# A place of its own for the fourth copy of a run's product sums, and the loads and sums that form z spread over the plain units

## The chip, the cores and the metric

The kernel runs on one core of one Trainium2 chip. The metric is the device time of one execution in microseconds (us); of several executions the median is taken. TensorE multiplies, VectorE and ScalarE work elementwise and empty the accumulator memory (PSUM), POOL (GpSimd) and SP issue transfers, and 16 DMA engines carry them. In the profile's rows PE is TensorE's matmuls, PEld its loading of the stationary operand, DVE is VectorE and ACT is ScalarE.

## What is computed

One layer of a hybrid decoder trunk on 512 positions of width 2048: a mixer of gated linear attention and mLSTM heads, then a feed-forward block with squared ReLU, both with a residual, a conditioning vector and a layer norm. The part that matters here is the end:

```python
def _sq_relu_mlp(u, w_ff1, w_ff2):
    return jnp.square(jax.nn.relu(u @ w_ff1)) @ w_ff2
...
        x = _layer_norm(ALPHA * x + g2 * y, ln2_g[l], ln2_b[l])
```

The hidden width is 8192, all data is float32. A float32 product is made of three products of rounded parts: each operand is split into hi (rounded) and lo (the rest), and hi·hi + hi·lo + lo·hi are accumulated.

## The kernel before, in words

The change lies in the second feed-forward product, from about 1500 to 2188 us: the hidden matrix h (kept in device memory as `hd`) times `w_ff2`. Its 8192 rows of depth are cut into pairs of 128-row tiles, the output's 2048 columns into four blocks b of 512 (`NCB`, `CB`). The list `units` sets the order of work; one unit is one pair times one block.

*Seven-product units* (kind "S", 96 of them, numbers 0 to 95). The first 24 pairs are multiplied by Strassen's scheme in Winograd's form: seven products of half-size operands in place of eight. `w_operands` (L1180 to L1198) makes a unit's weight operands: SP loads a raw weight tile into one of three buffers, ScalarE rounds a part of it (L1190, tiles named bh), VectorE forms combinations (`w_combos`, L1164 to L1167), ScalarE rounds those (L1194, hi), VectorE subtracts (L1197, bl; L1198, lo). This is done two units ahead (`LOOK`). `h_operands` makes a pair's seven operands of h (L1273 to L1284); they stay for as long as the pair is in use. `seven` (L1430 on) has 42 matmuls of 256 columns, six for each product, in the order 1, 2, 3, 7, 5, 6, 4 (`ORDER`).

Units come in 15 runs: run r works on block (r + 1) mod 4 with up to four groups of two pairs, so that the runs have 2, 4, 6, then nine times 8, then 6, 4 and 2 units. In the trace the runs begin at about 1500.1, 1511.5, 1538.1, 1574.9, 1615.3, 1657.7, and so on to 1974.5 (six units), 2008.3 (four) and 2030.8 (two). The seven products of a run are summed in seven of eight PSUM banks. At its end `evac` (L1452) copies them out: ScalarE copies two at a time into a staging place (L1457, seven copies into four places in turn), and a transfer carries each place to the block's `sums` in device memory: the first four runs write them plainly from SP's queue (L1462), later ones add to what is there, with accumulating transfers from POOL's queue (L1460). The staging places are three, used in rotation by `scratch("st", 2, 3)`: half-blocks of z that have no content yet. So the fourth staging of a run (product 4 alone) goes to the place of its first.

*Plain units* (kind "C", 24, numbers 96 to 119). The last pairs are multiplied without the scheme: six units a block, 24 matmuls of 512 columns each, from 2046.3 us on. Weights and h are split by `split` (L125, L126). In these units the function `at(n, fn)` puts side jobs ahead of unit n's matmuls, in the order in which they were registered: `sums_load` (L1469, seven loads of 256 KB from `sums` into tiles q), `z_sums` (L1471, seven operations of VectorE that turn a block's seven sums into its four quarters of z, in two steps), loads of the residual (`last_load`, L1403) and its scaling (`last_x2`, L1421 and L1422), layer-norm rows (`ln_rows`, L1122), the tail's operands (`tail_h`, `tail_w`) and, behind a block's last unit, the addition of its plain products to z (L1525) and `last_z` (L1426, L1427). Block 0's sums are loaded at unit 96 and summed at 97 and 98, block 1's at 99 to 101, block 2's at 102 to 104, block 3's at 105 to 107.

The tiles q, the residual, and 24 of the operands of eight pairs come from one ring of 28 places of 2 KB a partition (`f3_slot`, `NS`). The raw-weight buffers also take the layer-norm rows and the tail's raw tiles.

Order: `tc.manual_schedule(engines=MANUAL)` (L712) keeps VectorE and ScalarE in the order in which the source issues to them. TensorE, SP and POOL get their order from the planner, which may put an instruction ahead of others that it thinks late.

Of the kernel before, what the change touches and what calls it, by code (L numbers as in the profile page):

```python
# [13 lines left out]
ALU = mybir.AluOpType  # L14
# [3 lines left out]
S = 512  # L18
# [7 lines left out]
NCB = D // CB  # L26
# [32 lines left out]
def trunk_layer_kernel(  # L59
# [5 lines left out]
    V, A, T, G = nc.vector, nc.scalar, nc.tensor, nc.gpsimd  # L65
# [10 lines left out]
    def mm_bank(name, shape=(P, CB)):  # L76
        turns["mm"].append(turns["mm"].pop(0))
        kind = turns["mm"][-1]
        return psum.tile(list(shape), F32, tag=kind, bufs=6 if kind == "mm" else 2, name=name)
# [586 lines left out]
    for n, (i, g, k) in enumerate(units):  # L666
# [5 lines left out]
        if at_ == 0:  # L672
            gen = ada_start(*nxt) if nxt else iter(())
            steps = 4 * nxt[1] + 1 if nxt else 0
# [252 lines left out]
    st = zp.tile([P, NT, NCB, 6], F32, name="st")  # L927
    ab = zp.tile([P, 2, KT], F32, name="ab")

    def blk(b):  # L930
        return slice(b * CB, (b + 1) * CB)
# [134 lines left out]
    def f1_units(halves, banks, first=None, ahead=None):  # L1066
        for kp in range(KP):
# [23 lines left out]
    zs_ = [z[:, b, 2 * i:2 * i + 2].rearrange("p t c -> p (t c)")  # L1091
           for b in range(NCB) for i in range(2)]
    turn = {}

    def scratch(what, at, n):
        turn[what] = (turn.get(what, -1) + 1) % n
        return zs_[at + turn[what]]
# [21 lines left out]
    def ln_rows(g_ap, b_ap, b, name, tag="raw"):  # L1119
        gb = strm.tile([P, 2, CB], F32, tag=tag, bufs=3, name=name)  # L1120
        for i, ap in enumerate((g_ap, b_ap)):
            nc.sync.dma_start(gb[:, i, :], ap[0:1, blk(b)].broadcast_to([P, CB]))  # L1122
        return gb
# [46 lines left out]
    def halves(t):  # L1170
        return t.rearrange("p (e t) -> p e t", e=2)
# [57 lines left out]
    ORDER = (1, 2, 3, 7, 5, 6, 4)  # L1229
# [75 lines left out]
    NU = len(units)  # L1305
# [5 lines left out]
    def at(n, fn):  # L1311
        jobs.setdefault(n, []).append(fn)
# [5 lines left out]
    def prepare2(n):  # L1318
        if n < len(units):
            kind, b, ft, _, _ = units[n]  # L1320
            name = f"f2_{b}_{ft}"
            if kind == "S":
                ahead.append(w_operands(w_ff2, ft * P, b * CB, name, waiting, f1_slot))
            else:
                ahead.append(w_plain(ft * P, b * CB, name))


    for p in range(GP, SP + CP):
        use = [u[2] for u in units].index(2 * p)
        n = max(1, use - 6 + 3 * (p % 2)) if p < SP else NU - 10 + 2 * (p - SP)  # L1330
# [21 lines left out]
    for nb in range(2, DFF // CB):  # L1352
        pb = {m: mm_bank(f"fp{nb}_{m}", (P, 2, HB)) for m in ORDER}
# [44 lines left out]
    def f3_slot(name):  # L1398
        return ff3.tile([P, S], F32, tag="s", bufs=NS, name=name)

    def last_load(b, x2, t):
        x2.append(f3_slot(f"x2_{b}_{t}"))
        nc.sync.dma_start(x2[t], xd[t * P:(t + 1) * P, blk(b)])  # L1403
# [3 lines left out]
    def tail_h(i):  # L1407
        for h, l in h_operands("C", tail + 2 * i, "ssss"):
            act[0].append(h)
            act[1].append(l)  # L1410

    def tail_w(b, i):
        raw = raw_unit(w_ff2, (tail + 2 * i) * P, b * CB, CB, f"wl{b}_{i}")
        for t in range(2):
            V.tensor_tensor(raw[:, t, :], raw[:, t, :], g2b[b], ALU.mult)
        for t in range(2):
            w2[b, 2 * i + t] = h_split(raw[:, t, :], "hl", f"wl{b}_{i}_{t}_")


    def last_x2(x2, gb, t):  # L1420
        V.tensor_tensor(x2[t], x2[t], gb[:, 0, :], ALU.mult)  # L1421
        V.tensor_tensor(x2[t], x2[t], gb[:, 1, :], ALU.add)  # L1422

    def last_z(b, x2, t):
        zs = z[:, b, t]
        V.tensor_tensor(zs, zs, g2b[b], ALU.mult)  # L1426
        V.scalar_tensor_tensor(zs, x2[t], ALPHA, zs, ALU.mult, ALU.add)  # L1427
# [21 lines left out]
    sums = [hdram.tile([P, 7 * S], F32, name=f"sums{b}") for b in range(NCB)]  # L1449
    begun = set()  # L1450

    def evac(pb, b):  # L1452
        for i in range(0, 7, 2):
            ms = ORDER[i:i + 2]
            st_ = scratch("st", 2, 3)[:, :len(ms) * S]
            for e, m in enumerate(ms):
                A.copy(halves(st_[:, e * S:(e + 1) * S]), pb[m])  # L1457
            o = sums[b][:, i * S:(i + len(ms)) * S]
            if b in begun:
                G.dma_start(o, st_, accum_op=ALU.add)  # L1460
            else:
                nc.sync.dma_start(o, st_)  # L1462
        begun.add(b)


    def sums_load(b, q):
        for i, m in enumerate(ORDER):
            q[m] = f3_slot(f"q{b}_{m}")
            nc.sync.dma_start(q[m], sums[b][:, i * S:(i + 1) * S])  # L1469

    def z_sums(b, q):  # L1471
        c11, c12, c21, c22 = (z[:, b, 2 * i:2 * i + 2, o:o + HB] for i in range(2) for o in (HB, 0))
        p = {m: halves(t) for m, t in q.items()}
        V.tensor_tensor(c11, p[1], p[2], ALU.add)
        V.tensor_tensor(p[6], p[1], p[6], ALU.add)
        V.tensor_tensor(p[7], p[6], p[7], ALU.subtract)
        V.tensor_tensor(p[6], p[6], p[5], ALU.subtract)
        yield
        V.tensor_tensor(c12, p[3], p[6], ALU.subtract)
        V.tensor_tensor(c21, p[7], p[4], ALU.add)  # L1480
        V.tensor_tensor(c22, p[5], p[7], ALU.subtract)
        yield

    g2b = []
    for n, (kind, b, ft, first, last) in enumerate(units):
        if first and kind == "S":
            pb = {m: mm_bank(f"gp{n}_{m}", (P, 2, HB)) for m in ORDER}
        elif first:
            pb = [mm_bank(f"gp{n}_{t}") for t in range(NT)]
            if b == 0:  # L1490
                for i in range(NCB):
                    g2b.append(f3_slot(f"g2b{i}"))
                    nc.sync.dma_start(g2b[i], rowd[G2][0:1, blk(i)].broadcast_to([P, CB]))
            if b < 2:
                for i in range(2):
                    q = {}
                    at(n + 3 * i, lambda q=q, i=2 * b + i: sums_load(i, q))
                    steps = z_sums(2 * b + i, q)
                    for j in range(2):
                        at(n + 3 * i + 1 + j, lambda steps=steps: next(steps))  # L1500
            x2, gb = [], []
            at(n, lambda b=b, gb=gb: gb.append(ln_rows(ln1_g, ln1_b, b, f"ln1r{b}")))
            for t in range(NT):
                at(n + 1 + t, lambda b=b, x2=x2, t=t: last_load(b, x2, t))
                at(n + 2 + t, lambda x2=x2, gb=gb, t=t: last_x2(x2, gb[0], t))
            if b == 0:
                for i in range(2):
                    at(n + 3 + 2 * i, lambda i=i: tail_h(i))
            if b == 2:
                for i in range(2):  # L1510
                    at(n + 1 + 2 * i, lambda i=i: tail_w(0, i))
            if b == 3:
                for i in range(2, 7):
                    at(n - 1 + min(i, 5), lambda i=i: tail_w(i // 2, i % 2))
        for fn in jobs.pop(n, ()) if n < 3 else ():
            fn()
        prepare2(n + LOOK)
        for fn in jobs.pop(n, ()):
            fn()
        (seven if kind == "S" else plain)(pb, ahead.pop(0), hops[ft], first, last)  # L1520
        if last and kind == "S":
            evac(pb, b)
        elif last:
            for tt in range(NT):
                V.tensor_tensor(z[:, b, tt], z[:, b, tt], pb[tt], ALU.add)  # L1525
            for t in range(NT):
                at(n + 1 + t, lambda b=b, x2=x2, t=t: last_z(b, x2, t))
# [111 lines left out]
```

## Time and profile before

| what | us |
|---|---|
| median of three runs (lowest, highest) | 2239.55 (2236.37, 2242.37) |
| the profiled execution's own time | 2247.92 |
| its span, first to last instruction | 2246.2 |
| mean granted clock of TensorE, share of full | 0.987 |

The span is what the rows below are counted in; their times start at its first instruction. The profile tells, for each engine, when it was busy, how long it was idle ahead of an instruction, and which instruction or transfer ended that idle time (the releaser). Idle time of an engine costs something only where TensorE, or whatever ends last, waits for it in turn. Some matmul records are missing from the trace, so that counts of matmuls in a row are a little short.

### The profile page before, as it was taken

Reading aid. Unit: us, or ns where it says so; the run is one execution under the profiler, and the core shown is the slowest. Engines: PE = TensorE matmul, PEld = TensorE weight load, DVE = VectorE, ACT = ScalarE, POOL = GpSimd, SP = SyncE. Lnnn points to the kernel's source line nnn. Section 1 sums busy time; section 2 is a strip of 40 time slices with the busy share of each in tenths; the row PEclk is TensorE's granted clock in tenths of the full one; section 3 lists DMA queues with packets and bytes.
Section 4 is the critical chain, followed back from the end, with each engine's and each line's share of the span. In section 5 each row is a group of like instructions: output and inputs, shape, how many; then the busy total and the mean of one; then the engine's idle time right before and its main releaser. Section 6 shows DMA issues by size and latency. Waiting matters only on the chain.

```text
span 2246.2 us, 34969 instructions
## 1 busy us (share of the span) xinstructions
PE 2140.0 (95%) x13873; PEld 1942.7 (86%) x13873; DVE 1757.1 (78%) x2802; ACT 950.3 (42%) x1343; POOL 163.1 (7%) x151
## 2 busy tenths in 40 slices
PE   6989999999999999999999999999999998998997
PEld 4767788888887889999999999998999898997786
DVE  7986677678777798888878888797788878865788
ACT  3222644343331245445445454455544444444223
POOL 3334101000000000000000000000000010011002
PEclk9999999999999999999999999999999999999999
DMA  8875345666678866443444435455555566579752
GB/s 307 273 266 169 121 136 155 233 212 220 227 258 287 283 197 202 127 142 115 148 123 141 130 113 152 124 166 183 186 153 149 154 163 162 155 192 257 251 169 96
DMA packets 187087, 409.79 MB, mean 182 GB/s; under 512 B 17440, under 2 KB 19708, under 8 KB 186924
## 3 DMA queue, kind: packets, MB, share of 16 engines
q1 hardware_dynamic: 180588, 387.38, 53.0%
q0 software_dynamic: 6336, 20.19, 5.2%
q8 instruction: 108, 1.77, 0.3%
q14 instruction: 55, 0.45, 0.1%
HBM read 354.74 MB, written 52.71 MB: 181 GB/s over the span
## 4 chain that ended last, share of the span: by engine, by line
PE 56%; issue 18%; DVE 13%; DMA 8%; ACT 3%; POOL 1%; SPq 0%; ACTq 0%; POOLq 0%; DVEq 0%
PE fp L1362 8%; PE fp L1361 8%; PE fp L1363 8%; DMA wr<-in_w_ada_dram 3%; DVE wr L162 3%; DMA sums<-z 1%; PE wo_0b L228 1%; PE wo_0b L230 1%; PE wo_0b L229 1%; PE gp L1445 1%; PE gp L1444 1%; PE gp L1446 1%; DMA f<-in_w_ff_dram 1%; POOL sums L1460 1%; DVE z L1164 1%
## 5 line engine op out<-in xcount | busy, mean ns | idle before, releaser
L162 DVE SCALAR_TENSOR_TENSOR wr<-wr,csb 128x1024 f32<-128x1024 f32 x192 | 259.1, 1370 | 27.9 <-DMA wr<-in_w_ada_dram 27.7
L1164 DVE TENSOR_TENSOR z<-f 128x512 f32<-128x512 f32 x208 | 142.4, 685 | 0.0
L1460 POOL DMA_DIRECT2D sums<-z x44 | 37.9, 866 | 1175.3 <-DVE f_10lo L1198 813.9
L1166 DVE TENSOR_TENSOR z<-f,z 128x256 f32<-128x256 f32 x208 | 88.4, 425 | 7.2
L1167 DVE TENSOR_TENSOR z<-f,z 128x256 f32<-128x256 f32 x208 | 88.4, 425 | 7.2
L1457 ACT COPY z<-gp 128x512 f32<-128x512 f32 x105 | 54.2, 601 | 72.7 <-DMA sums<-z 61.5
L1387 ACT ACTIVATE z<-z 128x1024 f32<-128x1024 f32 x28 | 28.1, 1052 | 58.1 <-DVE z L1382 58.1
L1194 ACT CAST f_6hi<-z 128x1024 fp32r<-128x1024 f32 x18 | 18.9, 1051 | 39.2 <-DVE z L1167 39.2
L1198 DVE TENSOR_TENSOR f_0lo<-z,f_0hi 128x1024 fp32r<-128x1024 f32 x17 | 20.8, 1226 | 18.5 <-ACT f_0hi L1194 18.5
L1194 ACT CAST f_4hi<-z 128x1024 fp32r<-128x1024 f32 x18 | 18.9, 1053 | 33.8 <-DVE z L1167 33.8
L1194 ACT CAST f_0hi<-z 128x1024 fp32r<-128x1024 f32 x17 | 17.8, 1050 | 33.3 <-PE fp L1362 24.5
L654 DVE TENSOR_TENSOR gqk<-gqk,st 128x512 f32<-128x512 f32 x40 | 25.3, 679 | 7.5 <-PE st L223 7.4
L1198 DVE TENSOR_TENSOR f_1lo<-z,f_1hi 128x1024 fp32r<-128x1024 f32 x14 | 17.2, 1226 | 17.6 <-ACT f_1hi L1194 17.6
L654 DVE TENSOR_TENSOR gv<-gv,st 128x512 f32<-128x512 f32 x40 | 25.2, 679 | 6.2 <-PE st L230 6.2
L832 ACT ACTIVATE y<-mo,dd 128x256 f32<-128x256 f32 x16 | 7.6, 475 | 51.9 <-DVE dd L825 51.9
L126 DVE TENSOR_TENSOR ul<-uf,uh 128x512 fp32r<-128x512 f32 x16 | 11.9, 752 | 21.0 <-ACT uh L125 21.0
L1391 ACT ACTIVATE z<-z 128x1024 f32<-128x1024 f32 x28 | 28.0, 1049 | 0.0
L1194 ACT CAST f_5hi<-z 128x1024 fp32r<-128x1024 f32 x14 | 14.7, 1051 | 30.5 <-DVE z L1167 30.5
L1194 ACT CAST f_1hi<-z 128x1024 fp32r<-128x1024 f32 x14 | 14.7, 1050 | 29.7 <-PE fp L1362 24.5
L1194 ACT CAST f_7hi<-z 128x1024 fp32r<-128x1024 f32 x14 | 14.7, 1050 | 28.8 <-PE fp L1362 24.4
L1198 DVE TENSOR_TENSOR f_2lo<-z,f_2hi 128x1024 fp32r<-128x1024 f32 x18 | 22.1, 1226 | 5.8 <-ACT f_2hi L1194 5.8
L1198 DVE TENSOR_TENSOR f_6lo<-z,f_6hi 128x1024 fp32r<-128x1024 f32 x18 | 22.1, 1225 | 5.8 <-ACT f_6hi L1194 5.8
(1912 smaller groups left out, 9023.7 us busy)
## 6 DMA issues: line engine op xcount, KB each, us to landing
f<-in_w_ff_dram SPq DMA_DIRECT2D x232, 512.0 KB, 3.8
wr<-in_w_ada_dram SPq DMA_DIRECT2D x192, 512.0 KB, 4.6
sums<-z POOLq DMA_DIRECT2D x33, 512.0 KB, 8.5
hd<-z SPq DMA_DIRECT2D x32, 512.0 KB, 3.8
z<-hd SPq DMA_DIRECT2D x28, 512.0 KB, 4.1
q<-sums SPq DMA_DIRECT2D x28, 256.0 KB, 5.8
sums<-z SPq DMA_DIRECT2D x12, 512.0 KB, 4.8
z<-in_x_dram SPq DMA_DIRECT2D x4, 1024.0 KB, 5.2
```

The costliest lines, as they stand in the source:

```text
L162: V.scalar_tensor_tensor(raw, raw, 1.0, csb[:, h * DH:(h + 1) * DH], ALU.mult, ALU.mult, accum_out=msum[:, h, v * KT + k:v * KT + k + 1])
L654: V.tensor_tensor(o, o, src, ALU.add)
L1164: V.tensor_tensor(halves(f[:, :S]), halves(raw[:, HB:3 * HB]), b12.unsqueeze(1).to_broadcast([P, 2, HB]), ALU.add)
L1166: V.tensor_tensor(t2, b22, n1, ALU.add)
L1167: V.tensor_tensor(t4, b21, t2, ALU.add)
L1194: A.copy(th, f)
L1198: V.tensor_tensor(tl, f, th, ALU.subtract)
L1361: T.matmul(o, lhsT=wh[:, sl], rhs=q[:, 0], start=i == 0 and j == 0, stop=False)
L1362: T.matmul(o, lhsT=wh[:, sl], rhs=q[:, 1], start=False, stop=False)
L1363: T.matmul(o, lhsT=wl[:, sl], rhs=q[:, 0], start=False, stop=i == KP - 1 and j == 1)
L1457: A.copy(halves(st_[:, e * S:(e + 1) * S]), pb[m])
L1460: G.dma_start(o, st_, accum_op=ALU.add)
```

## The change

The fourth staging of a run gets a tile of its own from the ring of 28; the first three always take the half-blocks 2, 3 and 4 in order. `sums_load` takes a list of products, and a block's seven loads are issued in four portions (products 1 and 2; 6 and 7; 5; 3 and 4) at four units in a row. The seven operations of `z_sums` are the same, in three steps of two, three and two, one a unit: the quarter c22 is now formed in the second step. Block b's first loads are at unit 94 + 5b and its last step is at unit 98 + 5b, so block 0 begins two units earlier than before and block 3 ends six units later.

```diff
-    def evac(pb, b):
+    def evac(pb, b, n):
         for i in range(0, 7, 2):
             ms = ORDER[i:i + 2]
-            st_ = scratch("st", 2, 3)[:, :len(ms) * S]
+            st_ = zs_[2 + i // 2] if i < 6 else f3_slot(f"st{n}")
...
-    def sums_load(b, q):
-        for i, m in enumerate(ORDER):
+    def sums_load(b, q, ms):
+        for m in ms:
+            i = ORDER.index(m)
             q[m] = f3_slot(f"q{b}_{m}")
             nc.sync.dma_start(q[m], sums[b][:, i * S:(i + 1) * S])
...
-        p = {m: halves(t) for m, t in q.items()}
+        p = {}
+
+        def need(*ms):
+            p.update((m, halves(q[m])) for m in ms)
+
+        need(1, 2, 6)
         V.tensor_tensor(c11, p[1], p[2], ALU.add)
         V.tensor_tensor(p[6], p[1], p[6], ALU.add)
+        yield
+        need(7, 5)
         V.tensor_tensor(p[7], p[6], p[7], ALU.subtract)
         V.tensor_tensor(p[6], p[6], p[5], ALU.subtract)
-        yield
+        V.tensor_tensor(c22, p[5], p[7], ALU.subtract)
+        yield
+        need(3, 4)
         V.tensor_tensor(c12, p[3], p[6], ALU.subtract)
         V.tensor_tensor(c21, p[7], p[4], ALU.add)
-        V.tensor_tensor(c22, p[5], p[7], ALU.subtract)
-        yield
+        yield
+
+
+    for b in range(NCB):
+        q, n = {}, NU - 2 + 5 * b
+        steps = z_sums(b, q)
+        for i, ms in enumerate(((1, 2), (6, 7), (5,), (3, 4))):
+            at(n + i, lambda b=b, q=q, ms=ms: sums_load(b, q, ms))
+        for i in range(3):
+            at(n + 2 + i, lambda steps=steps: next(steps))
...
-            if b < 2:
-                for i in range(2):
-                    q = {}
-                    at(n + 3 * i, lambda q=q, i=2 * b + i: sums_load(i, q))
-                    steps = z_sums(2 * b + i, q)
-                    for j in range(2):
-                        at(n + 3 * i + 1 + j, lambda steps=steps: next(steps))
...
-            evac(pb, b)
+            evac(pb, b, n)
```

(`NU` is 96, the number of seven-product units.)

## Rows read from the trace of the kernel before

**Rows 1.** Page, part 1: busy us, share of the span, instructions

```profile
PE 2140.0 (95%) x13873; PEld 1942.7 (86%) x13873; DVE 1757.1 (78%) x2802; ACT 950.3 (42%) x1343; POOL 163.1 (7%) x151
```

**Rows 2.** Stretches: us, busy PE PEld DVE ACT POOL, clock, DMA share, GB/s

```profile
1538.10:1574.90 36.80, 32.44 (x254) 32.03 (x253) 30.37 (x48) 18.96 (x27) 0.00 (x0) 0.91 0.50 174
1574.90:1615.30 40.40, 40.40 (x339) 40.10 (x338) 33.46 (x51) 21.01 (x31) 0.00 (x0) 1.00 0.50 165
1615.30:1657.70 42.40, 40.74 (x339) 40.13 (x338) 35.65 (x55) 21.83 (x31) 0.00 (x0) 1.00 0.49 169
1657.70:1703.20 45.50, 41.26 (x339) 40.24 (x338) 35.63 (x55) 21.83 (x31) 3.69 (x4) 1.00 0.60 156
...
1930.00:1974.50 44.50, 41.92 (x338) 41.51 (x338) 35.59 (x55) 21.81 (x31) 3.41 (x4) 0.96 0.68 184
1974.50:2008.30 33.80, 31.66 (x254) 31.45 (x254) 24.73 (x37) 16.19 (x23) 3.46 (x4) 0.95 0.73 178
2008.30:2030.80 22.50, 20.71 (x171) 20.21 (x170) 14.17 (x20) 11.91 (x19) 3.40 (x4) 1.00 0.99 253
2030.80:2046.30 15.50, 11.72 (x87) 11.51 (x85) 5.07 (x9) 6.37 (x11) 3.32 (x4) 0.89 1.03 292
...
2144.40:2188.00 43.60, 43.60 (x194) 36.08 (x194) 36.79 (x53) 12.25 (x16) 0.00 (x0) 1.00 0.55 166
```

**Rows 3.** ScalarE's waits, 1495 to 2070: us in total, times, longest

```profile
ACT z L1457 <- DMA sums<-z: 61.5, 15, 6.8
```

**Rows 4.** Timeline of ScalarE, two run ends: start, us, instruction, [idle before]

```profile
1522.53 0.59 ACT L1457 COPY z<-gp 128x512 f32<-128x512 f32 x1 [2.78 <-DMA sums<-z]
...
1751.03 3.02 ACT L1457 COPY z<-gp 128x512 f32<-128x512 f32 x6
1759.24 0.59 ACT L1457 COPY z<-gp 128x512 f32<-128x512 f32 x1 [5.19 <-DMA sums<-z]
1759.72 0.84 ACT L1190 CAST f_20bh<-f 128x768 fp32r<-128x768 f32 x1
```

**Rows 5.** Timeline of VectorE behind the second of these

```profile
1760.59 0.96 DVE L1197 TENSOR_TENSOR f_20bl<-f,f_20bh 128x768 fp32r<-128x768 f32 x1 [6.69 <-ACT f_20bh L1190]
```

**Rows 6.** Timeline of TensorE: that run's end and the next run

```profile
1750.89 0.39 PE L1435 MATMUL gp<-f_18bl,h 128*128 128x256 f32 x1 [1.32 <-DVE f_18bl L1197]
1751.66 0.39 PE L1434 MATMUL gp<-f_16bh,h 128*128 128x256 f32 x1 [0.38 <-ACT z L1457]
...
1768.88 0.39 PE L1435 MATMUL gp<-f_22bl,h 128*128 128x256 f32 x1 [1.31 <-DVE f_22bl L1197]
```

**Rows 7.** POOL's accumulating transfers, all of them

```profile
DMA to landing us min/median/max: 6.0/8.2/12.8
```

**Rows 8.** Timeline of ScalarE at the last two run ends

```profile
2044.62 0.58 ACT L1457 COPY z<-gp 128x512 f32<-128x512 f32 x1 [6.82 <-DMA sums<-z]
...
2059.03 0.58 ACT L1457 COPY z<-gp 128x512 f32<-128x512 f32 x1 [4.89 <-DMA sums<-z]
2059.51 1.05 ACT L125 CAST f_52hi<-f 128x1024 fp32r<-128x1024 f32 x1
```

**Rows 9.** Timeline of TensorE: stalls in the plain units

```profile
2060.61 0.50 PE L1444 MATMUL gp<-f_52hi,hb 128*128 128x512 f32 x1 [1.84 <-ACT f_52hi L125]
2061.87 0.50 PE L1445 MATMUL gp<-f_52lo,hb 128*128 128x512 f32 x1 [0.76 <-DVE f_52lo L126]
...
2096.32 0.50 PE L1445 MATMUL gp<-f_52lo,hb 128*128 128x512 f32 x1 [1.30 <-DVE f_52lo L126]
...
2103.84 0.49 PE L1444 MATMUL gp<-f_54hi,hb 128*128 128x512 f32 x1 [2.01 <-ACT f_54hi L125]
2105.10 0.80 PE L1445 MATMUL gp<-f_54lo,hb 128*128 128x512 f32 x1 [0.77 <-DVE f_54lo L126]
```

**Rows 10.** Timelines of VectorE and SP's queue, second plain block

```profile
2083.20 0.68 DVE L1474 TENSOR_TENSOR z<-q,q 128x512 f32<-128x512 f32 x1
...
2091.96 3.37 SPq L1469 DMA_DIRECT2D q<-sums  x7
```

## The prediction

> **What bounds the kernel now.** I read the page first: TensorE is busy 95% of the span [rows 1], so the whole can only fall where it stands still. The change touches the second feed-forward product alone (1500 to 2188 us), so the next view is the table by stretch, one stretch per run of seven-product units, then who waits for whom on each engine, then the timelines round one run's end, last the timeline of the plain units.
>
> The table by stretch [rows 2] is the main finding. A run of eight units took 40.4 us once (the row of 1574.90), which is 5.05 us a unit, with TensorE busy throughout. The seven runs from 1657.70 to 1974.50 took 316.8 us, 45.3 each, with the same matmuls: 4.9 us of each is TensorE standing. VectorE is busy only 35.6 us of such a run, ScalarE 21.8, the DMA engines 0.60 to 0.68 of the time. No engine is full, so a wait sets the pace. Which one? ScalarE's copies out of PSUM (L1457) waited 61.5 us in 15 waits for the DMA that empties the staging place [rows 3]: three places rotate, a run makes four copies, and the fourth waits until the first one's accumulate has landed.
>
> One run's end shows how this reaches TensorE. ScalarE does six copies from 1751.03, stands 5.19 us, does the seventh at 1759.24, and only then the rounding f_20bh of a unit prepared ahead [rows 4]. VectorE needs f_20bh and stood 6.69 us for it, until 1760.59 [rows 5]. It is late from there on: TensorE stalls 1.31 us for its f_22bl at 1768.88; the run before ended with TensorE waiting 1.32 us for f_18bl and 0.38 us for a PSUM copy that ScalarE, held up behind f_18hi, had begun late [rows 6]. So the loop is VectorE's: 45.3 a run less the 6.69 wait leaves 38.6 us of its own work and short handshakes, and with the wait this is the period.
>
> **The change part by part.** *The fourth copy's own place.* It removes ScalarE's wait of 5.19 us in each run (all but a few of the 15 waits: the 61.5 us). The order of ScalarE and VectorE stays as written, so VectorE's wait falls by the same: 6.69 - 5.19 = 1.5 us stay, since seven copies and f_20bh still take longer than VectorE's work beside them. New VectorE loop: 38.6 + 1.5 = 40.1 us. TensorE alone needs 40.4 (the row of 1574.90, [rows 2]). So what is late next is TensorE itself, by 0.3 us, and I take 40.4 a run. The price is bounded below by that row's weight loading, 40.10 us (PEld), and above by the run of 1615.30, 42.4 us: its end still had a shorter wait, for plain writes in place of accumulates. I take 40.4 because it is the one row without a stall.
>
> The sum over the runs, all from [rows 2]: seven runs 316.8 - 7 x 40.4 = 34.0; the run of 1615.30, 42.4 - 40.4 = 2.0; six units, 33.8 - 30.3 = 3.5; four units, 22.5 - 20.2 = 2.3; two units, 15.5 - 10.6 = 4.9 (10.1 for two units, 0.5 left for a copy that is late; part of the loss here is a clock of 0.89 behind the stall, which goes with it); the six units of 1538.10 took 36.8, 6.5 over 30.3; the wait ahead of them, with a plain write, was 2.78 us [rows 4], so 2.8 of it goes. Together 49.5. By the upper price, 42.4 a run or 5.3 a unit, the seven save 20.0, the six, four and two units 2.0, 1.3 and 4.4, and with the 2.8 it is 30.5.
>
> The new place comes from the ring of 28 that also holds operands of the hidden matrix. Eight pairs take 24 of it, four runs four copies: just 28. The tile that had a place before is one of eight pairs back, last read by the unit that opened the previous run, eight units (40 us) ahead of the load, so nothing waits: cost 0, and if that cover were gone each load would hold ScalarE and VectorE (rival four). The fourth accumulate is issued by POOL right behind the third instead of 6 us later; nobody waits for it but the next use of its place, four runs on.
>
> *The last two runs' ends.* Here runs are short and accumulates slow (landing up to 12.8 us, [rows 7]): ScalarE waits 6.82 us, and at the very end in three steps, the longest 4.89 [rows 8]; f_52hi comes behind that at 2059.51, and TensorE stalls 1.84 and 0.76 us [rows 9]. The last run's first three copies now use the places of the run 10 us before. Accumulates that land after 6 us are gone by then, those that land after 12.8 are not, so up to some 3 us of wait stay; f_52hi would be done some 4 us after the plain units begin and is wanted at about 11. Gain 2.6, between 0 and 2.6.
>
> *Loads and sums spread.* No instruction is added or dropped: 28 loads and 28 VectorE operations of 0.68 us [rows 10]. Before, seven loads are asked for in one unit and four plus three sums in the next two; now the loads go two, two, one, two and the sums two, three, two, and they cover 20 units instead of 12. In the trace the burst costs this: four sums stand ahead of f_50lo, f_50lo frees the buffer of the next weight load, and seven loads in a row on SP's queue (3.37 us, [rows 10]) stand between that load and the next. TensorE then waits 1.30, 2.01 and 0.77 us [rows 9], and the clock is lower behind it. After the change no sum of that block stands ahead of f_50lo (four fewer, 2.7 us) and two instead of seven ahead of f_52lo (3.4 us); that covers the 1.30 and more than half of the rest. I take 3.5, between 0 and 6. Against it: the sums of the last block now fall in units 111 to 113, beside the weight preparation of the tail; there seven operations, 4.8 us, are new on VectorE, in a stretch where it is busy 36.79 of 43.60 us (the row of 2144.40, [rows 2]). Price: 0 to 2 us, I take 0.5. SP's queue is passed by loads that begin two units earlier (in the two-unit run); they wait for nothing that isn't done, but share engines that are full there (DMA share 1.03, [rows 2]).
>
> Sum: 49.5 + 2.6 + 3.5 - 0.5 = 55. The profiled execution took 2247.92 us (span 2246.2); the median of the runs is 2239.55, 8.4 less. Taking the same saving from the median gives 2184.5, say **2185**.
>
> **The rivals.** *Two: the stall at a run's end stays.* The order of TensorE is the planner's, not the source's: it put f_18's first product ahead of f_16's second [rows 6]. If VectorE is still a lap late there, TensorE loses some 1.5 to 2 us at each end, a period of 42.4. For: the stalls at the ends are as frequent as the others. Against: VectorE gains 5 us per run and needs two. Saving 30.5 + 5.6 = 36: 2203.
>
> *Three: the DMA engines take it back at the end.* The row of the two-unit run shows DMA share 1.03 at 292 GB/s, the one before 0.99, and all bytes of the last runs must now go in some 11 us less. Weight loads would land late, and the gains of the last three runs and the plain units (3.5 + 2.3 + 4.9 + 5.6 = 16) would go: 2201. In the long runs it can't: 0.60 to 0.68 of the time, times 45.3 / 40.4, is 0.67 to 0.76. The Trainium skill, "DMA: Bandwidth & Descriptors", section "Issuing engines are not separate DMA queues", says that transfers from all engines run on the same 16 and interleave; by that rule the fourth accumulate, brought forward on POOL's queue, takes from SP's weight loads as much as one on SP's own would. The trace agrees as far as the accumulates' landing spreads from 6.0 to 12.8 us.
>
> *Four, slower: the ring of 28 overfills.* Place: the two loads of hidden operands in each run. If a load's place were freed only by a unit of the run in progress, ScalarE and VectorE would stand behind it, in order. Up to about 5 us a run nothing is lost against before; at two waits of one unit (10 us) the loop is 50, 5 more than now, over nine runs some 45 us, less 6 saved elsewhere: 2279. It decides from more than 28 live places at the load; I count at most 28.
>
> *Five: the change doesn't do what it says.* The copy still waits, since its place belongs to a transfer under way. Only the plain units gain, 5.6: 2234, within 0.3%.
>
> **How the numbers follow.** Forecast 0.62, two 0.18, three 0.11, four 0.04, five 0.05. The forecast's own bounds: at 40.1 a run, with nothing left over in the two units, all 6.5 us of the run of 1538.10 and all 8.6 of the plain units' stalls, it is 36.1 + 2.3 + 3.7 + 2.4 + 5.5 + 6.5 + 8.6 = 65 saved, 2174; rival two without the plain units' gain saves 30.5, some 2209. The range 2174 to 2210 leaves out four, five and the ends of three: about 0.13. A measurement of this kernel can tell about 0.3%, 6.7 us, from no change. Forecast, two and three are all faster by more, 0.91; five is the same, 0.05; four slower, 0.04.
>
> **What would show it.** Right: no wait of L1457 for the DMA beyond the last run; VectorE's wait for f_20bh's like near 1.5 us; runs of eight units at 40 to 41 us; no stall for "bl" tiles from the second accumulate on; the q loads two by two. Wrong: runs of 42 us with the wait at a run's start (two); weight roundings waiting for their loads after 1990 us (three); a wait in front of the hidden operands' rounding (four); L1457 still waiting 5 us (five).

## The result, and the profile after

The changed kernel took 2178.78 us (median of 4 runs, 2175.23 to 2185.78), the kernel before, run beside it, 2240.96 (2236.37 to 2243.6): a ratio of 0.9728, 95% interval 0.9698 to 0.9758, or 62 us less. 2185 was predicted. The profiled execution took 2177.70 us (span 2176.0).

First the page's busy line of the kernel after, to be read against [rows 1]:

```profile
PE 2116.9 (97%) x13873; PEld 1929.2 (89%) x13873; DVE 1753.3 (81%) x2802; ACT 949.7 (44%) x1343; POOL 164.7 (8%) x151
```

The same 13873 matmuls, and a span 70.2 us shorter (2246.2 against 2176.0). Of that, 8.6 us lie ahead of anything that was changed: the seven-product units began at 1500.1 before and at 1491.5 after. That is scatter of single executions: in the kernels below, all the same up to there, they began anywhere from 1490.0 to 1499.2. It may also be why the profiled execution of before lay above its median; the other executions left no trace to show it. The stretches that the change touches account for the other 61.6: the seven-product stretch went from 546.2 to 489.6 us (-56.6), the plain units from 141.6 to 136.6 (-5.0).

The table by stretch of the kernel after, same columns as [rows 2]: the third run (six units), the fifth and the eighth (eight units each), the last three (six, four and two units), and the plain units:

```profile
1529.80:1561.60 31.80, 30.34 (x254) 30.01 (x253) 27.91 (x42) 17.82 (x26) 0.00 (x0) 1.00 0.58 190
1601.50:1641.40 39.90, 39.90 (x338) 39.90 (x337) 35.52 (x55) 21.61 (x32) 0.00 (x0) 1.00 0.54 178
1721.20:1761.10 39.90, 39.90 (x338) 39.90 (x337) 35.52 (x55) 21.60 (x32) 3.44 (x4) 1.00 0.67 179
1921.10:1951.10 30.00, 30.00 (x254) 29.95 (x253) 26.11 (x38) 18.84 (x30) 4.40 (x6) 1.00 0.82 214
1951.10:1971.10 20.00, 20.00 (x171) 20.00 (x170) 15.64 (x22) 13.23 (x21) 4.11 (x5) 1.00 1.02 256
1971.10:1981.10 10.00, 10.00 (x87) 10.00 (x86) 3.66 (x4) 4.74 (x8) 2.73 (x4) 1.00 1.03 262
1981.10:2117.70 136.60, 133.93 (x578) 109.99 (x578) 104.17 (x146) 36.25 (x45) 2.59 (x3) 0.98 0.76 240
```

A run of eight units is 39.9 us where it was 45.3, and TensorE never stands: the weight loading (PEld) is as long as the window, and in the trace no matmul of these runs starts later behind the one before it than the usual 0.12 us. The runs of six, four and two units have come down to their matmuls' time too, with the DMA engines as full in the last two (1.02 and 1.03) as before.

Next ScalarE's wait, the row that answers [rows 3], from the view of waits:

```profile
ACT z L1457 <- DMA sums<-z: 4.8, 2, 2.7
```

61.5 us in 15 waits have become 4.8 in 2, both at the end of the last run. And one run's end, the timelines of ScalarE and of VectorE that answer [rows 4] and [rows 5]:

```profile
1720.84 3.01 ACT L1457 COPY z<-gp 128x512 f32<-128x512 f32 x6
1723.69 0.64 ACT L1457 COPY st<-gp 128x512 f32<-128x512 f32 x1
1724.17 0.89 ACT L1190 CAST f_20bh<-f 128x768 fp32r<-128x768 f32 x1
```

```profile
1725.09 0.96 DVE L1197 TENSOR_TENSOR f_20bl<-f,f_20bh 128x768 fp32r<-128x768 f32 x1 [1.39 <-ACT f_20bh L1190]
...
1765.11 0.96 DVE L1197 TENSOR_TENSOR f_24bl<-f,f_24bh 128x768 fp32r<-128x768 f32 x1 [1.39 <-ACT f_24bh L1190]
```

Seven copies and the rounding follow each other without a pause, and VectorE waits 1.39 us for them instead of 6.69. The two VectorE lines are one run apart: its loop is 40.02 us.

The stalls of [rows 9] are gone. One new one stands in the plain units, at f_56, the weights of the first block's fifth unit; on TensorE's timeline, with its cause on ScalarE's:

```profile
2005.02 0.61 PE L1444 MATMUL gp<-f_56hi,hb 128*128 128x512 f32 x1 [2.02 <-ACT f_56hi L125]
2006.28 0.80 PE L1445 MATMUL gp<-f_56lo,hb 128*128 128x512 f32 x1 [0.65 <-DVE f_56lo L126]
```

```profile
2003.92 1.04 ACT L125 CAST f_56hi<-f 128x1024 fp32r<-128x1024 f32 x1 [12.14 <-DMA f<-in_w_ff_dram]
```

### The profile page after: what moved, and what is told of

Read it like the earlier page. It is cut to its first block, busy times and chain, and to the rows that moved or that the text cites. A ratio compares the mean times of both kernels' runs of the same rounds, so it can differ in the third digit from the quotient of the medians.

```text
span 2176.0 us, 34974 instructions
## 1 busy us (share of the span) xinstructions
PE 2116.9 (97%) x13873; PEld 1929.2 (89%) x13873; DVE 1753.3 (81%) x2802; ACT 949.7 (44%) x1343; POOL 164.7 (8%) x151
## 4 chain that ended last, share of the span: by engine, by line
PE 74%; DVE 13%; DMA 8%; ACT 2%; issue 2%; POOL 0%; SPq 0%; ACTq 0%; DVEq 0%; POOLq 0%
PE fp L1362 8%; PE fp L1361 8%; PE fp L1363 8%; PE gp L1434 7%; PE gp L1435 7%; PE gp L1436 7%; DVE wr L162 3%; DMA wr<-in_w_ada_dram 3%; DMA f<-in_w_ff_dram 2%; PE wo_0b L228 1%; PE wo_0b L230 1%; PE wo_0b L229 1%; DMA q<-sums 1%; PE mv0b L228 1%; PE gr0b L228 1%
## 5 line engine op out<-in xcount | busy, mean ns | idle before, releaser
L1460 POOL DMA_DIRECT2D sums<-z x33 | 28.5, 867 | 1110.3 <-DVE f_10lo L1198 802.2
L1457 ACT COPY z<-gp 128x512 f32<-128x512 f32 x90 | 45.5, 603 | 5.8 <-DMA sums<-z 4.8
L1194 ACT CAST f_6hi<-z 128x1024 fp32r<-128x1024 f32 x18 | 18.9, 1052 | 39.3 <-DVE z L1167 39.3
```

The costliest lines, as they stand in the source:

```text
L1194: A.copy(th, f)
```

## The experiments

**Which half of the change carries the gain.** *The place alone:*

```diff
-            st_ = scratch("st", 2, 3)[:, :len(ms) * S]
+            st_ = zs_[2 + i // 2] if i < 6 else f3_slot(f"st{n}")
```

> Only the fourth copy of a run gets its own place (a slot of the ring of 28); loads and sums of z stay as before. My theory: ScalarE's wait of 5.2 us in front of the fourth copy is the pace of every run's end, and it alone carries the gain. Every run of eight units should come down to 39.9 us from about 45, so the stretch of seven products (546.2 us before, 489.6 after the change) should be 487 to 492 us, and the two TensorE stalls of the plain units near f_52 and f_56 stay: 5 us more than the changed kernel there. Time 2183 to 2190. Rival (the gain needs both parts, because the bunched z loads hold the additions up): the stretch stays over 510 us, time over 2205.

It took 2193.64 us, ratio 0.9771 (0.9746 to 0.9797). The table by stretch, one run of eight units and the plain units:

```profile
1723.20:1763.10 39.90, 39.90 (x339) 39.90 (x338) 35.53 (x55) 21.62 (x32) 3.34 (x5) 1.00 0.69 179
1982.50:2126.90 144.40, 137.49 (x578) 111.65 (x577) 104.62 (x146) 35.16 (x43) 2.30 (x3) 0.95 0.75 232
```

The seven-product stretch is 490.4 us (1492.1 to 1982.5), as my theory has it; the rival that needs both halves falls. The median is 4 us above what I expected. The profiled execution, at 2185.52 us the shortest of the four, is inside the range, but its plain units are already 2.8 us longer than before, 144.4 against 141.6. There the stall at f_52 that stands first in [rows 9] is gone, and TensorE stands 3.13 and 0.46 us at f_56 instead. SP's queue shows what lies ahead of f_56's load:

```profile
1982.60 16.77 SPq L1469 DMA_DIRECT2D q<-sums  x7
2000.36 0.38 SPq L130 DMA_DIRECT2D f<-in_w_ff_dram  x1
```

The seven loads of block 0's sums take 16.8 us to be issued, and the next weight load stands behind them. In the kernel before, the planner had put these seven ahead, one or two at a time between 2013.49 and 2030.4, in the last seven-product units; the first of them, on SP's queue before:

```profile
2013.49 1.12 SPq L1469 DMA_DIRECT2D q<-sums  x2
```

So spreading them is worth more once the place is there: 144.4 - 136.6 = 7.8 us.

*The spread alone* (the diff of the change without its `evac`):

```diff
+        for i, ms in enumerate(((1, 2), (6, 7), (5,), (3, 4))):
+            at(n + i, lambda b=b, q=q, ms=ms: sums_load(b, q, ms))
+        for i in range(3):
+            at(n + 2 + i, lambda steps=steps: next(steps))
```

> Only the loads and sums of z are spread over the plain units; the fourth copy still waits for the first of three rotating places. My theory: the runs keep about 45 us each and the seven-product stretch stays at 546 us within 3; the plain units lose at most the 5 us that the changed kernel lost there. Time 0 to 6 us under the kernel before (2233 to 2241). Rival (spreading carries much of the gain): more than 15 us under it.

2238.84 us, ratio 0.9982 (0.9965 to 0.9999). The waits of ScalarE and the table by stretch:

```profile
ACT z L1457 <- DMA sums<-z: 66.9, 16, 6.5
```

```profile
1740.70:1786.10 45.40, 42.40 (x339) 41.77 (x338) 35.67 (x55) 21.83 (x32) 3.42 (x4) 0.96 0.61 157
2036.70:2173.80 137.10, 133.20 (x579) 109.14 (x579) 107.50 (x151) 38.91 (x50) 3.41 (x4) 0.99 0.76 224
```

The runs keep their 45 us, and ScalarE still waits, 66.9 us in all; only the plain units are 4.5 us shorter. By the medians the two halves alone save 49 and 4 us, and both in one kernel 62, each with an interval of 4 to 7 us to either side. The traces give 53.0, 4.0 and 61.6 us for the two stretches.

**Is the wait the pace of a run, or is TensorE's order?** *The wait lengthened:* two rotating places instead of three.

```diff
-            st_ = scratch("st", 2, 3)[:, :len(ms) * S]
+            st_ = scratch("st", 2, 2)[:, :len(ms) * S]
```

> The kernel before with two rotating places instead of three, so that the third and the fourth copy both wait for an addition to land. My theory (the wait at the places sets the pace of a run's end): ScalarE waits about 8 us a run in place of 5.2, and each of some eleven runs gets about 2.8 us longer; with the shorter runs 25 to 40 us slower, 2265 to 2280. Rival two of the prediction (TensorE's order at a run's end sets the pace, the wait is covered): within 5 us of the kernel before.

2275.68 us, ratio 1.0149 (1.0122 to 1.0177). One run's end on ScalarE, and VectorE behind it:

```profile
1802.03 2.04 ACT L1457 COPY z<-gp 128x512 f32<-128x512 f32 x4
1810.11 1.07 ACT L1457 COPY z<-gp 128x512 f32<-128x512 f32 x2 [6.04 <-DMA sums<-z]
1812.86 0.59 ACT L1457 COPY z<-gp 128x512 f32<-128x512 f32 x1 [1.68 <-DMA sums<-z]
```

```profile
1814.21 0.96 DVE L1197 TENSOR_TENSOR f_24bl<-f,f_24bh 128x768 fp32r<-128x768 f32 x1 [9.31 <-ACT f_24bh L1190]
```

ScalarE stands 6.04 + 1.68 = 7.7 us where it stood 5.2, VectorE 9.3 where it stood 6.7, and the run from 1799.3 to 1847.2 is 47.9 us where it was 45.3. Each rose by 2.5 to 2.6: the wait goes into the period in full. This is one run; over the seven long runs VectorE's wait rose from 6.7 to 9.6 us on average, and the period from 45.3 to 48.2.

*TensorE's order taken from the planner* (the kernel before, the source's order for TensorE from the seven-product units on):

```diff
+    region.__exit__(None, None, None)
+    region = tc.manual_schedule(engines=MANUAL | {mybir.EngineType.PE})
+    region.__enter__()
     g2b = []
```

> The kernel before, but TensorE's instructions of the seven-product stretch go in the order of the source, so that no product of the second unit is put ahead at a run's end. My theory: the order of TensorE is a follower, and ScalarE's wait for a place ends last either way: within 6 us of the kernel before, runs of 45 us as they were. Rival two (the order is the cause): a good part of the gain comes with it, at least 20 us faster, eight-unit runs of 42 us or less.

2245.3 us, ratio 1.001 (0.9993 to 1.0027). One run in the table by stretch, its start on TensorE, and VectorE in it:

```profile
1791.50:1836.90 45.40, 40.67 (x339) 40.06 (x337) 35.60 (x55) 21.82 (x31) 3.42 (x4) 1.00 0.63 156
```

```profile
1794.56 0.39 PE L1434 MATMUL gp<-f_20bh,h 128*128 128x256 f32 x1 [2.22 <-ACT z L1457]
```

```profile
1803.68 0.96 DVE L1197 TENSOR_TENSOR f_24bl<-f,f_24bh 128x768 fp32r<-128x768 f32 x1 [6.87 <-ACT f_24bh L1190]
```

The stall moves to the run's start, where TensorE waits 2.22 us for the copies, and the period stays 45.4: the order decides where TensorE stands, not how long. The kernel before says so too. In its runs at 1884.7 and 1930.0 the planner put nothing ahead, and they took 45.3 and 44.5 us. What rules out rival two of the prediction itself, a stall that stays after the change, is the 39.9 us of the runs after. (There the planner no longer puts the second unit ahead from the fourth run on.)

*The fourth copy moved, with no place added:* three rotating places and bunched loads as before, but the fourth copy comes two units into the next run.

```diff
-            evac(pb, b)
+            evac(pb, b, (0, 2, 4))
+            at(n + 2, lambda pb=pb, b=b: evac(pb, b, (6,)))
```

> No place is added: the kernel before with its three rotating places and its bunched z loads, but a run's fourth copy is issued two units (about 10 us) into the next run, when the first addition has landed. My theory (ScalarE standing at the place, with the splits of the next run queued behind it, is the whole loss): the runs of eight units come to 39.9 to 40.5 us as with the own place, seven-product stretch 487 to 495 us, time 2180 to 2196. Rival (the fourth place itself is what gains, by letting the additions be issued at once): runs stay over 42 us, time over 2205. As it takes no slot of the ring of 28, its plain units tell whether the 144.5 us of the run with the own place alone came from the slot: then they are 142 or less here; if from the additions' transfers, about 144.

2189.28 us, ratio 0.9768 (0.9747 to 0.9789). ScalarE's timeline at one run's end, and the table by stretch:

```profile
1757.42 3.32 ACT L1457 COPY z<-gp 128x512 f32<-128x512 f32 x6
1760.64 0.84 ACT L1190 CAST f_24bh<-f 128x768 fp32r<-128x768 f32 x1
...
1769.93 0.58 ACT L1457 COPY z<-gp 128x512 f32<-128x512 f32 x1
```

```profile
1760.70:1800.60 39.90, 39.90 (x339) 39.90 (x338) 35.63 (x54) 22.01 (x33) 3.42 (x4) 1.00 0.68 178
1980.10:2121.50 141.40, 134.94 (x578) 109.85 (x577) 102.09 (x143) 35.29 (x44) 3.40 (x4) 0.98 0.70 213
```

The copy finds its place free at 1769.93, and the runs are 39.9 us without any new place. So it isn't memory that gains, it is that ScalarE, which goes in the order of the source, doesn't stand with the next run's roundings behind it.

**What is late next.** The changed kernel with the seventh copy made six times more, TensorE in source order:

```diff
                 A.copy(halves(st_[:, e * S:(e + 1) * S]), pb[m])
+                for _ in range(6 if i == 6 else 0):
+                    A.copy(halves(st_[:, e * S:(e + 1) * S]), pb[m])
```

> The changed kernel with its seventh copy made six times more at each run's end (about 3.0 us of ScalarE, by its timeline, where six copies took 3.01 us), and TensorE in source order so that the planner's reaction to the longer end does not mix in. It asks what is late next behind the wait that went. My theory: VectorE's loop (about 40.0 us a run, with 1.39 us of waiting for the rounding behind the copies) is as long as TensorE's 39.9, so there is nothing left to hide in: VectorE's wait at a run's end becomes 4.4 us, eight-unit runs 42.5 to 43.1 us once VectorE's lead is used up, and the seven-product stretch 508 to 522 us in place of 489.6. Rival (TensorE alone is the bound and VectorE has room): runs stay at 40 to 40.5, stretch under 496.

2226.23 us, ratio 0.9935 (0.9909 to 0.996). ScalarE, VectorE and the table by stretch:

```profile
1753.29 3.67 ACT L1459 COPY st<-gp 128x512 f32<-128x512 f32 x6
```

```profile
1757.73 0.96 DVE L1197 TENSOR_TENSOR f_20bl<-f,f_20bh 128x768 fp32r<-128x768 f32 x1 [5.11 <-ACT f_20bh L1190]
```

```profile
1747.50:1791.20 43.70, 41.70 (x339) 41.50 (x338) 35.67 (x55) 25.23 (x37) 3.42 (x4) 0.96 0.66 163
```

The six copies took 3.67 us, not 3.0: repeated from one bank into one place they follow each other more slowly than six different ones. VectorE's wait rose by 5.11 - 1.39 = 3.72 us and the run by 43.7 - 40.0 = 3.7. So the mechanism was right and the size of the added work was wrong, and with it the stretch: 534.4 us, outside the 508 to 522. I had also let a lead of VectorE absorb more than it does. It shows in the first run of eight only:

```profile
1574.30:1616.30 42.00, 40.49 (x339) 40.09 (x338) 34.05 (x52) 25.07 (x37) 0.00 (x0) 1.00 0.49 160
1616.30:1660.00 43.70, 40.50 (x339) 40.09 (x338) 35.67 (x55) 25.25 (x37) 0.00 (x0) 1.00 0.49 163
```

That the loop is VectorE's, with ScalarE, and that TensorE follows, shows in who waits for whom. In the seven runs from the sixth on, VectorE waits for ScalarE alone and never for TensorE: 62.7 us in 56 waits before, 26.2 in 56 after, 51.4 in 56 here. TensorE stands at the runs' starts here, for the first copies (L1457), which ScalarE makes ahead of the added ones. So after the change nothing is left to hide in at a run's end, as far as one size of added work can show: 3.7 us more on ScalarE cost 3.7 us a run.

**Rival four, the ring.** The changed kernel with two slots fewer:

```diff
-    NS, SP, GP, CP = 28, 24, 2, 6
+    NS, SP, GP, CP = 26, 24, 2, 6
```

> The changed kernel with a ring of 26 slots in place of 28, a test of rival four of the prediction. By my count the tile that has a slot before is last read some seven units (35 us) ahead of the load that wants it, still with two fewer, so the runs stay at 39.9 us and the seven-product stretch at 489 to 492; the plain units, which take x2, q and g2b from the same ring, get 0 to 4 us longer. Rival four (the ring is used to its last slot, and a load that finds none holds ScalarE and VectorE): eight-unit runs over 42 us, stretch over 505.

2182.9 us, ratio 0.9743 (0.9709 to 0.9777). One run and the plain units:

```profile
1760.40:1800.30 39.90, 39.90 (x339) 39.90 (x338) 35.54 (x55) 21.61 (x32) 3.45 (x4) 1.00 0.69 179
1980.40:2117.50 137.10, 133.74 (x578) 109.82 (x577) 104.26 (x146) 36.26 (x45) 2.66 (x4) 0.98 0.78 243
```

Nothing moved: the runs are 39.9 us, the stretch 489.7. That just 28 places are in use, as I had counted, is no limit on the pace of the runs: two fewer cost nothing there.

**The new stall at 2005 us.** Four row loads, g2b, are asked for at the first plain unit. The trace has the landing of one of the four. By the view of that tile it came 5.1 us after its issue before; after:

```profile
DMA to landing us min/median/max: 18.9/18.9/18.9
```

The view of SP's waits, 1960 to 2060 us, tells how this reaches f_56. The load of its weights, the one that SP issued at 1993.85, stood 2.8 us until a g2b row had landed, and then took some 10 us itself:

```profile
SPq L130 <- DMA g2b<-row: 4.4, 2, 2.8
```

```profile
1993.85 0.38 SPq L130 DMA_DIRECT2D f<-in_w_ff_dram  x1
```

The changed kernel was run again beside two kernels that move the rows:

> The changed kernel once more, beside the three that differ from it by a few microseconds: 2172 to 2186 us.

2181.47 us, ratio 0.9742 (0.9722 to 0.9763); plain units 135.6 us, with the stall at f_56hi again (2.04 and 0.76 us).

*Spread over plain units 2 to 5:*

```diff
+    for i in range(NCB):
+        at(NU + 2 + i, lambda i=i: g2b_load(i))
...
-            if b == 0:
-                for i in range(NCB):
-                    g2b.append(f3_slot(f"g2b{i}"))
-                    nc.sync.dma_start(g2b[i], rowd[G2][0:1, blk(i)].broadcast_to([P, CB]))
```

> The changed kernel, with the four row loads g2b spread over plain units 2 to 5 rather than asked for together at the first. My theory of its stall near 2005 us (f_56's weights land late because the g2b rows, landing about 19 us after issue, and the q loads crowd the DMA engines from 1978 to 2003): the stall of 2.0 and 0.65 us and the 6.8 us at the half clock behind it go, so the plain units take 130 to 134 us in place of 136.6, time 3 to 6 us under the changed kernel. Rival (f_56's load waits for a slot of the ring, not for the DMA engines): stall and time stay within 2 us.

2179.3 us, ratio 0.9725 (0.9703 to 0.9746). ScalarE's rounding of that weight, and the plain units:

```profile
2010.11 1.05 ACT L125 CAST f_56hi<-f 128x1024 fp32r<-128x1024 f32 x1 [8.08 <-DMA f<-in_w_ff_dram]
```

```profile
1989.70:2123.80 134.10, 131.69 (x579) 107.84 (x578) 101.60 (x142) 34.93 (x43) 2.59 (x3) 1.00 0.77 238
```

Two of the rows, those whose landing the trace has, land after 12.4 and 6.7 us; no weight load waits for one any more, and f_56's goes out 8.1 us into the plain units in place of 12.8. ScalarE's wait falls from 12.14 (10.66 in the second execution) to 8.08, TensorE stands 0.57 us there in place of 2.7. A stall of 1.51 us is new, though, at f_52lo in the second block: the stalls of the plain units add up to 2.4 us where they were 2.7, so the 1.5 to 2.5 us by which the plain units are shorter lie mostly elsewhere; the granted clock is 1.00 for 0.98 and 0.99. In the time of the whole it can't be told from the changed kernel, and the 3 to 6 us that I expected were too many.

*Six units earlier:* the same loads at `at(NU - 4, ...)`.

> The changed kernel, with the four g2b rows asked for at unit 92, six units before the plain units. My theory: as with the spread rows, the crowd near 1980 us is gone and the plain units get 3 to 6 us shorter; the four ring slots are then held for 30 us longer, and if the ring is what runs short, a weight load of the last runs waits and 2 to 5 us are lost in the seven-product stretch (490 us becomes 492 to 495).

2180.62 us, ratio 0.9731 (0.9714 to 0.9748). The stretch stays at 489.6, and the plain units don't get the 3 to 6 us shorter that I expected: 135.2 us. A like stall appears one weight earlier, at f_54hi (2.19 and 0.76 us). So the rows were what f_56's load stood behind, but the crowd is there without them: take them out and another weight load is late.

*All together without a slot:* the late fourth copy, the spread loads and sums, the late rows.

> The gains put together without a slot of the ring: the fourth copy two units late into one of the three rotating places, the z loads and sums spread as in the change, the g2b rows spread over plain units 2 to 5. Runs 39.9 us, stretch 489 to 491. If the slot of the fourth copy is what the plain units of the changed kernel pay for, they come to 130 to 133 us against 134.0 with the rows spread alone, and the time to 2172 to 2178; if the transfers are, to 134 to 136 us and 2176 to 2183.

2179.59 us, ratio 0.9723 (0.9703 to 0.9743). The table by stretch:

```profile
1768.50:1808.40 39.90, 39.90 (x339) 39.90 (x337) 35.64 (x54) 22.03 (x33) 3.43 (x5) 1.00 0.70 179
1987.90:2124.90 137.00, 133.34 (x578) 109.07 (x577) 103.12 (x145) 36.73 (x47) 3.41 (x4) 0.99 0.73 226
```

The plain units are longer than either expectation: 137.0. This kernel takes no slot for the copy, so nothing here speaks for the slot as what the plain units pay for, though the 141.4 against 144.4 us of the late copy and the place alone had looked like it. But neither comparison is clean, because the planner moved the g2b rows in each. With the place alone they went at 1980.5 to 1982.1, into the crowd, and with the late copy at 1905.8 to 1909.4, 71 to 74 us ahead of the plain units. Here the first two of the four went 21 and 10 us ahead of the plain units, and not inside them as the source has it. What the last 2 or 3 us of the plain units depend on stays open. No kernel tried is measurably faster than the changed one.

## Why the prediction was right

It said 2185 and 2178.78 came, a saving of 55 us against 62 by the medians. Step by step:

- *The bound.* That ScalarE's wait for the staging place sets the pace, by way of VectorE, was right. It was shown from three sides: remove the wait (by a place or by a later copy) and the period is 39.9; lengthen it by 2.5 us and the period grows by 2.6; put 3.7 us of work where it was and the period grows by 3.7.
- *VectorE's wait falls to 1.5 us:* 1.39. *Its loop 40.1:* 40.02.
- *TensorE's price of a run, 40.4 us:* a little too high, 39.9. The row of 1574.90 in [rows 2] looked free of stalls since its busy time filled the window, but four of its matmuls began late, by 0.43 us in all, counted from the starts in the trace, and the profile counted these as busy. Its PEld of 40.10, my lower bound, was not one either. The price enters eight times: seven runs gave 37.1 us for 34.0, the run of 1615.30 gave 2.5 for 2.0.
- *What is late next:* I named TensorE, with 0.3 us to spare on VectorE. They are level, 39.9 and 40.0, and the added copies show that VectorE's loop counts as soon as it gets longer.
- *Six, four and two units:* 3.8, 2.5 and 5.5 us for 3.5, 2.3 and 4.9. The clock's part went with the stalls, as said: 1.00 in all three.
- *The run of 1538.10:* 5.0 us for 2.8 in the profiled execution, but this is a place where executions differ. In the other kernels that have the place or the late copy, without added copies, it took 31.8 to 34.3 us, and in the second execution of the changed kernel 35.6, a saving of 1.2, at a granted clock of 0.90 behind a stall of 2.67 us:

```profile
1535.30:1570.90 35.60, 32.93 (x255) 32.72 (x254) 31.20 (x48) 20.77 (x31) 0.00 (x0) 0.90 0.58 187
```

- *Plain units, last runs' ends:* 2.6 + 3.5 - 0.5 = 5.6 were forecast, 5.0 came, and 6.0 in the second execution (141.6 - 135.6). That the sum fits is in part luck. The place did take away f_52's stall, as the 2.6 has it, but alone it made the plain units 2.8 us longer, with a new stall of 3.6 us at f_56. The spread alone took away the stalls of the second block and gave 4.5 us for 3.0, and together with the place it also repaid what the place had cost. No term of the forecast has the stall at f_56, of which 2.7 us stay. One number of the working is no reading: the stalls of [rows 9] add up to 6.7 us, and the 8.6 in the range's lower end is the sum of the two upper bounds, 2.6 and 6.
- *Rival three* had named that stall's sign, weight roundings that wait for their loads after 1990 us. The sign alone doesn't tell much, since ScalarE's roundings waited for loads in the plain units before too (26.0 us at f_54hi). What came is small: the gains of the last three runs were not lost, though the DMA share of the last two is 1.02 and 1.03. The accumulates do land later than in [rows 7], but nobody waits for them except twice in the last run; from the view of their line, after:

```profile
DMA to landing us min/median/max: 5.7/10.7/14.9
```

By the Trainium skill, "DMA: Bandwidth & Descriptors", section "Issuing engines are not separate DMA queues", transfers run on the same 16 engines whichever engine started them. The trace doesn't speak against it: a g2b row took 5.1 us to land before, and 18.9 where POOL's accumulates and SP's loads were under way together. No run tells POOL's part in that from the part of SP's own loads.

- *Rivals two, four and five* did not happen: TensorE's order followed, the ring had room, the wait was gone.

By the two profiled executions the terms are 37.1 + 2.5 + 3.8 + 2.5 + 5.5 + 5.0 = 56.4 for the 49.5 of the sum over the runs, and 5.0 for 5.6 behind them, together 61.4 for 55.1. The largest part of the difference is the price of a run; 2.2 us of it are the run of 1538.10, where executions differ.

## What to carry to other kernels

Where an engine that goes in order waits for a buffer, ask what is queued behind it and who needs that; here a wait ahead of one short copy held up another engine's input, and the whole wait went into the period. Then ask whether the waiting step can simply come later: two units later was worth as much in the runs as one more buffer. And a stretch in which the busy time fills the window isn't yet free of waits: take the price of a step from the spacing of its instructions.

## What the runs showed that I had not expected

- Six copies in a row took 3.01 us from changing banks into changing places, and 3.67 us where one bank was copied into one place six times. Which of the two matters was not tried.
- Of the same four row loads, the one whose landing the trace has landed 5.1 us after its issue where they went 77 to 81 us ahead of the plain units (before), and 18.9 us where they went at most 2 us ahead, into the crowd (after). The change doesn't touch them; that they moved is the planner's doing, and why it moved them was not tried.
- Two executions of the same kernel differ by 3.8 us in one run of six units (31.8 and 35.6), where a stall at the run's start was 1.46 us in one and 2.67 in the other, and the granted clock 1.00 and 0.90.
